# Low weight parts by an accumulating DMA instead of a GpSimd subtraction, in a two-layer hybrid decoder

## The chip, the cores and the metric

The kernel runs on one core of a Trainium2 chip. A core has a matrix engine (TensorE, PE in the profile, with its weight loads on a row of their own, PEld), a vector engine (VectorE, DVE), a scalar engine (ScalarE, ACT), GpSimd (POOL), and SyncE (SP), which here only issues DMAs. ACT and POOL can issue DMAs too. Each engine runs its own list of instructions in order and waits at semaphores for the others. The metric is the device time of one execution in microseconds; the kernel before takes 1241.17 us (median of 3 runs, 1240.09 to 1242.71).

## The reference

Two decoder layers on 512 tokens of width 1024, in float32. A layer has four groups of attention heads that share one input projection and one output projection, then a dense feed-forward network, with a norm ahead of and behind each part:

```python
for l in range(DEPTH):                      # DEPTH = 2
    h = rmsnorm(x, g_pre_mix[l])
    z = jnp.einsum('bsd,de->bse', h, w_in[l])
    z_moba, z_fox, z_fg, z_cq, z_ckv, z_kr, z_dil = jnp.split(z, SPLIT_POINTS, axis=-1)
    ...
    mix = jnp.concatenate([from_heads(o_moba), from_heads(o_fox), from_heads(o_mla),
                           from_heads(o_dil)], axis=-1)
    y = jnp.einsum('bse,ed->bsd', mix, w_out[l])
    x = x + rmsnorm(y, g_post_mix[l])
    h = rmsnorm(x, g_pre_ffn[l])
    f = jax.nn.silu(jnp.einsum('bsd,df->bsf', h, w_gate[l])) * jnp.einsum('bsd,df->bsf', h, w_up[l])
    f = jnp.einsum('bsf,fd->bsd', f, w_down[l])
    x = x + rmsnorm(f, g_post_ffn[l])
```

The latents (`z_fg`, `z_cq`, `z_ckv`, `z_kr`; 356 columns) feed the forget gates and the low-rank attention.

## The kernel before, in words

**Matmuls in three passes.** Every float32 operand of a projection is split into a high part `hi` (the value cast to `float32r`, a type that the matrix engine multiplies faster) and a low part `lo = value - hi`. `mm3` (L195 to L198) multiplies hi·hi, hi·lo and lo·hi into one PSUM bank. So each weight chunk that is loaded costs a load, a cast and a subtraction before all three passes can run.

**Weight chunks.** `weights()` (L159 to L173) makes one chunk, mostly 128 x 512 values (256 KB). SyncE loads it into a buffer `wraw` (L166; there are 5, `WRAW`), ACT casts it (L167) into `whi` or a place given by `into`, and the low part is made from `wraw` and `hi`, either on DVE (L172) or on GpSimd (L170). `wlo` and `whi` have 6 buffers each (`WSPL`). `chunk_no` counts the chunks, and every chunk whose number is a multiple of `pool_share` goes to GpSimd: every 4th in the front of a layer (`SHARE_MIX`), every 10th while attention runs (`SHARE_HEADS`), every 2nd in the first feed-forward blocks (`SHARE_FFN`), and none after them. In the two layers that makes 26 chunks: 18 `wlo`, 4 `lat_lo` (the latent projection's weights, 128 x 356), 2 `w_half`, 1 `wlate`, 1 `wfirst`. A buffer `wraw` is free for the load five chunks later when both its readers are done.

**Order of the work.** The five engines' lists come from a scheduler that runs when the kernel is built and orders the instructions by costs of its own, so a change of one instruction can move others. At the very start it is switched off for ACT, DVE and POOL, and the order is written by hand, in a string of steps "s0 a0 w0 w1 t0 s1 w2 w3 a1 s2 t1 a2 s3 t2 a3 t3" (L1027): for the four row blocks of 128 tokens, `s` is the norm's statistics (ACT L230, then two small POOL instructions for the reciprocal root, L234 and L235), `a` the scaling on DVE (L209) and the transposes on PE (`hnT`, L217), and `t` the split of the transposed rows into `h` (cast on ACT and subtraction on DVE, both L225). The steps w0 to w3 load the four chunks of the first value projection; the fourth of them is a GpSimd chunk (`wlo_185`).

**The head.** PE computes the value projection `ps_v` and the latent projection `ps_lat` of one row block after the other as `h` comes. The latents need eight weight chunks, k = 0 to 7, whose high parts are `lat_hi` and whose low parts lie in two tiles: `lat_lo_265` for k = 0 to 3 and `lat_lo_266` for k = 4 to 7. Chunks k = 3 and k = 7 are GpSimd chunks.

**Behind the head.** The projections of the head groups, attention, and the output projection `ps_out` (weights `wearly`, `wlate`, `wlo`) run interwoven. Then comes the feed-forward network: its first blocks (`ps_g`, `ps_u`) start while the last row blocks of the output projection are still closed with norms (L764 to L767), and the rest is a long chain of matmuls in which all low parts come from DVE.

Of the kernel before, what the change touches and what calls it, by code (L numbers as in the profile page):

```python
# [13 lines left out]
ALU = mybir.AluOpType  # L14
# [62 lines left out]
def f32(ap):  # L77
    return ap.bitcast(F32)
# [3 lines left out]
def decoder(ctx, tc, x, positions, w_in, b_forget, g_mla_q, w_mla_q_up, g_mla_kv, w_mla_kv_up,  # L82
            w_out, g_pre_mix, g_post_mix, w_gate, w_up, w_down, g_pre_ffn, g_post_ffn, consts, out):
    nc = tc.nc
# [71 lines left out]
    chunk_no = [0]  # L156
    pool_share = [SHARE_MIX]

    def weights(src, shape, into=None):  # L159
        raw = wp.tile([P] + shape, F32, name="wraw", tag="wraw", bufs=WRAW)  # L160
        if into is None:
            hi = wp.tile([P] + shape, F32R, name="whi", tag="whi", bufs=WSPL)
            lo = wp.tile([P] + shape, F32R, name="wlo", tag="wlo", bufs=WSPL)
        else:
            hi, lo = into
        nc.sync.dma_start(raw, src)  # L166
        nc.scalar.copy(hi, raw)  # L167
        chunk_no[0] += 1
        if pool_share[0] and chunk_no[0] % pool_share[0] == 0:
            nc.gpsimd.tensor_tensor(lo, raw, f32(hi), op=ALU.subtract)  # L170
        else:
            nc.vector.tensor_tensor(lo, raw, f32(hi), op=ALU.subtract)  # L172
        return hi, lo  # L173
# [16 lines left out]
    def weights_v(l, c0, i, into=None):  # L190
        return weights(w_cols(l, c0, 256, 2 * i, 2), [2, 256], into=into)
# [76 lines left out]
    def mixing(l, h_in, in_slots, out_slots, w_first, turns_in):  # L268
# [43 lines left out]
        def fetch_T(c0):  # L312
            return [weights(w_cols(l, c0, P, 4 * i, 4), [4, P]) for i in range(2)]
# [230 lines left out]
        def window(col):  # L544
# [7 lines left out]
        lat_hi = keep.tile([P, KD, N_LAT], F32R, name="lat_hi", tag="slotE")  # L552
        lat_lo = [slot(s, F32R, "lat_lo") for s in out_slots[1:3]]
        wl = [weights(w_in[l, k * P:(k + 1) * P, C_LAT:C_LAT + N_LAT], [N_LAT],
                      into=(lat_hi[:, k, :], lat_lo[k // 4][:, k % 4, 0:N_LAT])) for k in range(KD)]
        gains_lat = R(F32, "gqkv")
# [537 lines left out]
```

## Time and profile before

| | |
|---|---|
| median of 3 runs | 1241.17 us (1240.09 to 1242.71) |
| profiled execution | 1241.33 us |
| span of its trace | 1239.5 us |
| PE busy | 1211.5 us, 98% |
| DVE busy | 890.6 us, 72% |
| ACT busy | 666.9 us, 54% |
| POOL busy | 245.0 us, 20% |

The span is what the trace shows from the first to the last instruction; 1.8 us of the profiled execution's time lie around it. Busy times of different engines overlap. A row of a timeline gives the start and the duration in microseconds, the engine, the line, the operation with what it writes and reads, the number of like instructions in a row, and in brackets how long the engine stood idle before it and whose end it waited for. In the lines of the profile of before `ACT L167` is the cast of a weight chunk, `POOL L170` the subtraction on GpSimd and `DVE L172` the subtraction on DVE.

### The profile page before, as it was taken

What the parts mean: (1) busy time and instruction counts of PE and PEld (TensorE: products, weight loads), DVE (VectorE), ACT (ScalarE), POOL (GpSimd) and SP (SyncE); (2) the same over time, 40 slices, a digit from 0 to 9 for tenths busy, and PEclk for the clock granted to TensorE, in tenths of its full rate; (3) what the DMA queues carried; (4) which work ended last, traced back from release to release, by engine and by line L of the source; (5) the groups of instructions that cost most, each with busy time, mean ns of one, the idle gap of its engine ahead of it and who ended that gap; (6) DMA issues with size and microseconds to landing.
All of it is one profiled execution on the core that took longest, in us unless ns stands there. A gap on an engine that the chain in (4) does not pass through costs nothing.

```text
span 1239.5 us, 20756 instructions
## 1 busy us (share of the span) xinstructions
PE 1211.5 (98%) x7372; PEld 1069.6 (86%) x7372; DVE 890.6 (72%) x1802; ACT 666.9 (54%) x1453; POOL 245.0 (20%) x337
## 2 busy tenths in 40 slices
PE   8999999989999999999999999999899999999997
PEld 7878877779999999888798888778799999998886
DVE  6877877778987888533667678766788987893334
ACT  6676766754554445332547677666454444453232
POOL 3343444343000000000242434333420000000001
PEclk9999999999999999999999999999999999999999
DMA  7221242521433333533622123233224333343331
GB/s 233 76 61 43 70 117 71 162 68 35 135 96 103 111 103 94 152 95 102 186 84 52 43 69 98 73 116 106 69 69 129 111 94 103 104 117 113 102 91 71
DMA packets 158060, 121.68 MB, mean 98 GB/s; under 512 B 9090, under 2 KB 133122, under 8 KB 157956
## 3 DMA queue, kind: packets, MB, share of 16 engines
q1 hardware_dynamic: 151908, 111.55, 30.9%
q10 hardware_dynamic: 6048, 8.80, 2.7%
q8 instruction: 58, 0.95, 0.3%
q14 instruction: 46, 0.38, 0.1%
HBM read 111.93 MB, written 4.19 MB: 94 GB/s over the span
## 4 chain that ended last, share of the span: by engine, by line
PE 83%; DVE 6%; ACT 4%; issue 2%; DMA 2%; POOL 2%; ACTq 0%; DVEq 0%; POOLq 0%
PE ps L197 8%; PE ps L196 8%; PE ps L198 8%; PE ps_d L197 6%; PE ps_d L198 6%; PE ps_d L196 6%; PE ps_g L197 4%; PE ps_g L196 4%; PE ps_g L198 3%; PE ps_qk L196 3%; PE ps_s L462 3%; PE ps_qk L197 3%; PE ps_qk L198 3%; PE pT L486 2%; PE ps_o L494 1%
## 5 line engine op out<-in xcount | busy, mean ns | idle before, releaser
L172 DVE TENSOR_TENSOR wlo<-wraw,whi 128x512 fp32r<-128x512 f32 x206 | 156.2, 767 | 133.2 <-ACT whi L167 130.7
L167 ACT CAST whi<-wraw 128x512 fp32r<-128x512 f32 (+1 forms) x224 | 135.7, 620 | 170.7 <-PE ps_d L198 117.9
L895 ACT CAST whi<-wsum 128x512 fp32r<-128x512 f32 x120 | 74.3, 620 | 133.4 <-DVE wsum L901 46.5
L197 PE MATMUL ps<-sum,whi 128*128 128x256 f32 x480 | 135.8, 283 | 0.0
L196 PE MATMUL ps<-sum,whi 128*128 128x256 f32 x480 | 135.5, 282 | 0.0
L198 PE MATMUL ps<-sum,wlo 128*128 128x256 f32 x480 | 135.3, 282 | 0.0
L196 PE MATMUL ps_d<-whi,fh 128*128 128x512 f32 x288 | 112.2, 390 | 0.0
L197 PE MATMUL ps_d<-wlo,fh 128*128 128x512 f32 x288 | 112.1, 389 | 0.0
L198 PE MATMUL ps_d<-whi,fl 128*128 128x512 f32 x288 | 112.0, 389 | 0.0
L198 PE MATMUL ps<-h,wlo 128*128 128x256 f32 x360 | 101.9, 283 | 0.0
L197 PE MATMUL ps<-h,whi 128*128 128x256 f32 x360 | 101.9, 283 | 0.0
L196 PE MATMUL ps<-h,whi 128*128 128x256 f32 x360 | 101.8, 283 | 0.0
L477 POOL TENSOR_SCALAR pr<-pr,den 128x128 f32<-128x128 f32 (+3 forms) x128 | 75.7, 608 | 115.1 <-DVE den L474 85.2
L198 PEld LDWEIGHTS ps<-sum,wlo 128*128 128x128 f32 x480 | 91.9, 192 | 0.0
L196 PEld LDWEIGHTS ps<-sum,whi 128*128 128x128 f32 x480 | 91.8, 191 | 0.0
L197 PEld LDWEIGHTS ps<-sum,whi 128*128 128x128 f32 x480 | 91.8, 191 | 0.0
L896 DVE TENSOR_TENSOR wlo<-wsum,whi 128x512 fp32r<-128x512 f32 x120 | 80.9, 683 | 9.5 <-ACT whi L895 8.4
L197 PE MATMUL ps_g<-h,whi 128*128 128x512 f32 (+1 forms) x224 | 81.3, 363 | 5.8 <-DVE h L225 5.8
L196 PE MATMUL ps_g<-h,whi 128*128 128x512 f32 (+1 forms) x224 | 81.1, 363 | 0.9 <-ACT h L225 0.8
L198 PE MATMUL ps_g<-h,wlo 128*128 128x512 f32 (+1 forms) x224 | 80.6, 360 | 0.0
L895 ACT CAST whi<-wraw 128x512 fp32r<-128x512 f32 x90 | 55.8, 620 | 42.6 <-PE ps L197 27.5
L196 PE MATMUL ps_qk<-h,whi 128*128 128x512 f32 x192 | 76.5, 398 | 0.0
(330 smaller groups left out, 3437.8 us busy)
## 6 DMA issues: line engine op xcount, KB each, us to landing
wraw<-in_w_gate_dram SPq DMA_DIRECT2D x88, 256.0 KB, 3.5
wraw<-in_w_up_dram SPq DMA_DIRECT2D x88, 256.0 KB, 3.1
wraw<-in_w_down_dram SPq DMA_DIRECT2D x88, 256.0 KB, 2.9
wraw<-in_w_in_dram SPq DMA_DIRECT2D x72, 256.0 KB, 3.1
wraw<-in_w_out_dram SPq DMA_DIRECT2D x32, 256.0 KB, 2.8
xt<-in_x_dram SPq DMA_DIRECT2D x16, 256.0 KB, 3.7
rope_b<-rope_a ACTq DMA_DIRECT2D x64, 64.0 KB, 2.0
wraw<-in_w_in_dram SPq DMA_DIRECT2D x16, 178.0 KB, 2.9
```

Source lines behind the costliest of these rows:

```text
L167: nc.scalar.copy(hi, raw)
L172: nc.vector.tensor_tensor(lo, raw, f32(hi), op=ALU.subtract)
L196: nc.tensor.matmul(ps, a_hi, b_hi, start=start, stop=False)
L197: nc.tensor.matmul(ps, a_hi, b_lo, start=False, stop=False)
L198: last_mm[0] = nc.tensor.matmul(ps, a_lo, b_hi, start=False, stop=stop)
L462: nc.tensor.matmul(ps[:, 0:w], a[:, qt * P:(qt + 1) * P], b[:, 0:w], start=i == 0, stop=i == n - 1)
L477: nc.gpsimd.tensor_scalar(p, p, den[:, t - qa:t - qa + 1], 1.0, op0=ALU.mult, op1=ALU.mult)
L486: nc.tensor.transpose(pt[:, i * P:(i + 1) * P], pr[:, offs[qt] + kt * P:offs[qt] + (kt + 1) * P], ident)
L494: nc.tensor.matmul(o, v, mh, start=kt == 0, stop=False)
L895: nc.scalar.copy(hi, raw)
L896: nc.vector.tensor_tensor(lo, raw, f32(hi), op=ALU.subtract)
```

## The change

The subtraction on GpSimd goes. In its place ACT writes the negated value of the raw chunk, cast to `float32r`, into the low tile (so -hi), and GpSimd issues a DMA that reads the raw chunk and adds it to what stands in the low tile: raw - hi. All 26 chunks take this way; those of DVE stay. Everything from L159 on stands four lines lower in the changed kernel.

```diff
@@ -156,6 +156,10 @@
     chunk_no = [0]
     pool_share = [SHARE_MIX]
 
+    def low_by_dma(lo, raw):
+        nc.scalar.mul(lo, raw, -1.0)
+        nc.gpsimd.dma_start(lo, raw, accum_op=ALU.add)
+
     def weights(src, shape, into=None):
@@ -167,7 +171,7 @@
         nc.scalar.copy(hi, raw)
         chunk_no[0] += 1
         if pool_share[0] and chunk_no[0] % pool_share[0] == 0:
-            nc.gpsimd.tensor_tensor(lo, raw, f32(hi), op=ALU.subtract)
+            low_by_dma(lo, raw)
         else:
             nc.vector.tensor_tensor(lo, raw, f32(hi), op=ALU.subtract)
         return hi, lo
```

The scheduler puts the new instructions into the engines' lists, and with that others move. Three places follow.

First, ACT in the head, from the cast of the last chunk of the value projection on. `wraw_279` and `wraw_295` are the latent chunks k = 3 and k = 7 before, `wraw_280` and `wraw_297` the same now; `hnT_219` and `hnT_220` is the first half of row block 2, `hnT_247` and `hnT_248` that of row block 3, and the next `hnT` after each the second half. Before:

```order
L167 CAST whi_184<-wraw_183 128x512
L230 ACTIVATE hn_206,ss_205<-xt_201 128x512
...
L167 CAST lat_hi_264<-wraw_279 128x356
L167 CAST lat_hi_264<-wraw_283 128x356
L167 CAST lat_hi_264<-wraw_287 128x356
L225 CAST h_123<-hnT_219 128x4x128
...
L167 CAST lat_hi_264<-wraw_295 128x356
L167 CAST whi_554<-wraw_553 128x512
L167 CAST whi_560<-wraw_559 128x512
L225 CAST h_123<-hnT_247 128x4x128
L225 CAST h_124<-hnT_252 128x4x128
```

And now:

```order
L171 CAST whi_184<-wraw_183 128x512
L160 ACTIVATE wlo_185<-wraw_183 128x512
L234 ACTIVATE hn_207,ss_206<-xt_202 128x512
...
L171 CAST lat_hi_265<-wraw_280 128x356
L160 ACTIVATE lat_lo_266<-wraw_280 128x356
L229 CAST h_123<-hnT_220 128x4x128
...
L171 CAST lat_hi_265<-wraw_297 128x356
L229 CAST h_123<-hnT_248 128x4x128
L160 ACTIVATE lat_lo_267<-wraw_297 128x356
L229 CAST h_124<-hnT_253 128x4x128
```

The three negations stand between the casts; the one of k = 7 stands between the two casts of row block 3, where before it was POOL's work behind the cast of k = 7.

Second, PE in the head, where it comes to the latent chunk k = 3 and to the transposes of row block 3. Before (`lat_lo_265` holds k = 0 to 3, `lat_lo_266` k = 4 to 7):

```order
L196 MATMUL ps_lat_330<-lat_hi_264,h_123 128x356
L197 MATMUL ps_lat_330<-lat_lo_265,h_123 128x356
L198 MATMUL ps_lat_330<-lat_hi_264,h_125 128x356
L196 MATMUL ps_lat_330<-lat_hi_264,h_124 128x356
L197 MATMUL ps_lat_330<-lat_lo_266,h_124 128x356
...
L217 MATMUL hnT_247<-cst_79,hn_234 128x128 x4
L197 MATMUL ps_v_365<-wlo_185,h_124 128x256
L198 MATMUL ps_v_365<-whi_184,h_126 128x256
L217 MATMUL hnT_252<-cst_79,hn_235 128x128 x4
L197 MATMUL ps_lat_330<-lat_lo_266,h_124 128x356
```

And now (`lat_lo_266` holds k = 0 to 3, `lat_lo_267` k = 4 to 7):

```order
L200 MATMUL ps_v_368<-whi_184,h_124 128x256
L201 MATMUL ps_lat_333<-lat_lo_266,h_123 128x356
L221 MATMUL hnT_248<-cst_79,hn_235 128x128 x4
L202 MATMUL ps_lat_333<-lat_hi_265,h_125 128x356
L200 MATMUL ps_lat_333<-lat_hi_265,h_124 128x356
L221 MATMUL hnT_253<-cst_79,hn_236 128x128 x4
L201 MATMUL ps_lat_333<-lat_lo_267,h_124 128x356
...
L200 MATMUL ps_lat_395<-lat_hi_265,h_123 128x356
L201 MATMUL ps_lat_395<-lat_lo_266,h_123 128x356
L201 MATMUL ps_lat_333<-lat_lo_267,h_124 128x356
```

The pass with the low part of k = 3 now stands right ahead of the transposes of row block 3, where before most of the passes of k = 4 to 6 and of the value projection lay between them; the last row shown is the pass with the low part of k = 7.

Third, ACT in the output projection of layer 0, around one chunk of `w_out` (`wraw_2945` before, `wraw_2953` now). Before:

```order
L541 CAST mix_2632<-mixf_2782 128x256
L488 CAST ptb0_95<-pT_2886 128x384
L756 COPY park_2739<-ps_out_2830 128x512
L167 CAST whi_2946<-wraw_2945 128x512
L167 CAST whi_2952<-wraw_2951 128x512
```

And now:

```order
L171 CAST whi_2954<-wraw_2953 128x512
...
L760 COPY park_2747<-ps_out_2773 128x512
L160 ACTIVATE wlo_2955<-wraw_2953 128x512
L171 CAST whi_2961<-wraw_2960 128x512
...
L545 CAST mix_2640<-mixf_2790 128x256
...
L492 CAST ptb0_95<-pT_2894 128x384
L760 COPY park_2747<-ps_out_2838 128x512
```

The cast and the negation of this chunk stand ahead of the copy of the next `ps_out` bank, where before the cast stood behind it.

## Rows read from the trace of the kernel before

**Rows 1.** The page's first lines: busy time of each engine with its share of the span and its instructions.

```profile
span 1239.5 us, 20756 instructions
PE 1211.5 (98%) x7372; PEld 1069.6 (86%) x7372; DVE 890.6 (72%) x1802; ACT 666.9 (54%) x1453; POOL 245.0 (20%) x337
```

**Rows 2.** The waits of PE by what it waited for: total us, times, longest us.

```profile
PE ps_g L197 <- DVE h L225: 5.8, 4, 1.9
...
PE ps_out L197 <- POOL wlo L170: 0.4, 1, 0.4
```

**Rows 3.** The GpSimd subtraction, L170, by the tile that it writes (count, shortest/median/longest ns), and one row of the cast of a weight chunk on ACT from the groups by line (count, busy us, mean ns).

```profile
L170 POOL TENSOR_TENSOR wlo<-wraw,whi x18: 1282/1298/1832, 12.7 to 873.7; 128x512 fp32r<-128x512 f32 x18
...
L167 ACT CAST lat_hi<-wraw 128x356 fp32r<-128x356 f32 x16 | 7.3, 489 | 3.5 <-DMA wraw<-in_w_in_dram 3.3
L167 ACT CAST whi<-wraw 128x512 fp32r<-128x512 f32 (+1 forms) x224 | 135.7, 620 | 170.7 <-PE ps_d L198 117.9
```

**Rows 4.** The timeline of the head: ACT, POOL, DVE, then PE.

```profile
11.53 1.13 ACT L167 CAST whi<-wraw 128x512 fp32r<-128x512 f32 x2
17.34 1.65 ACT L167 CAST lat_hi<-wraw 128x356 fp32r<-128x356 f32 x4
21.83 0.49 ACT L167 CAST lat_hi<-wraw 128x356 fp32r<-128x356 f32 x1 [1.21 <-DMA wraw<-in_w_in_dram]
25.58 1.07 ACT L225 CAST h<-hnT 128x512 fp32r<-128x512 f32 x2
...
12.73 1.29 POOL L170 TENSOR_TENSOR wlo<-wraw,whi 128x512 fp32r<-128x512 f32 x1
18.45 1.04 POOL L170 TENSOR_TENSOR lat_lo<-wraw,lat_hi 128x356 fp32r<-128x356 f32 x1
22.40 0.95 POOL L170 TENSOR_TENSOR lat_lo<-wraw,lat_hi 128x356 fp32r<-128x356 f32 x1 [2.91 <-ACT lat_hi L167]
...
14.31 0.97 DVE L172 TENSOR_TENSOR lat_lo<-wraw,lat_hi 128x356 fp32r<-128x356 f32 x2
...
14.07 0.39 PE L197 MATMUL ps_v<-wlo,h 128*128 128x256 f32 x1 [0.18 <-POOL wlo L170]
21.11 0.28 PE L198 MATMUL ps_v<-whi,h 128*128 128x256 f32 x1
21.23 0.28 PE L196 MATMUL ps_v<-whi,h 128*128 128x256 f32 x1
22.31 0.63 PE L217 MATMUL hnT<-cst,hn 128*128 128x128 f32 x4
24.21 0.32 PE L196 MATMUL ps_lat<-lat_hi,h 128*128 128x356 f32 x1
24.37 0.33 PE L197 MATMUL ps_lat<-lat_lo,h 128*128 128x356 f32 x1
```

**Rows 5.** DMA issues of the first 30 us (the first two rows), and of the whole run (the others): KB each, median us from issue to landing.

```profile
wraw<-in_w_in_dram SPq DMA_DIRECT2D x8, 256.0 KB, 3.8
wraw<-in_w_in_dram SPq DMA_DIRECT2D x8, 178.0 KB, 3.0
...
rope_b<-rope_a ACTq DMA_DIRECT2D x64, 64.0 KB, 2.0
out_dram<-xt SPq DMA_DIRECT2D x8, 256.0 KB, 2.0
gain<-in_g_post_ffn_dram ACTq DMA_DIRECT2D x4, 256.0 KB, 5.9
```

**Rows 6.** A stretch of the head: busy time and instructions of PE, PEld, DVE, ACT and POOL, the granted clock, the busy share of the DMA engines, GB/s.

```profile
20.00:25.00 5.00, 4.75 (x34) 4.34 (x33) 4.22 (x8) 1.73 (x4) 0.95 (x1) 1.00 0.82 209
```

**Rows 7.** The timeline where a GpSimd chunk of the first projections of layer 0 is made, and the PE row that reads it first.

```profile
43.11 1.46 POOL L170 TENSOR_TENSOR wlo<-wraw,whi 128x512 fp32r<-128x512 f32 x1 [4.13 <-ACT whi L167]
...
52.51 0.39 PE L198 MATMUL ps_qk<-h,wlo 128*128 128x512 f32 x1
```

**Rows 8.** The timeline of the chunk `wraw_2945` of the output projection in layer 0.

```profile
238.82 1.67 ACT L167 CAST whi<-wraw 128x512 fp32r<-128x512 f32 x3
...
239.53 1.29 POOL L170 TENSOR_TENSOR wlo<-wraw,whi 128x512 fp32r<-128x512 f32 x1 [0.55 <-ACT whi L167]
...
240.88 0.50 PE L197 MATMUL ps_out<-wlo,mix 128*128 128x512 f32 x1 [0.37 <-POOL wlo L170]
```

**Rows 9.** The timeline at the start of the feed-forward network of layer 0.

```profile
266.62 1.28 POOL L170 TENSOR_TENSOR w_half<-wraw,w_half 128x512 fp32r<-128x512 f32 x1 [1.23 <-ACT w_half L167]
...
267.19 1.25 DVE L764 TENSOR_TENSOR park<-park,gain 128x512 f32<-128x512 f32 x1 [0.66 <-ACT jk L230]
...
268.37 0.68 DVE L225 TENSOR_TENSOR h<-hnT,h 128x512 fp32r<-128x512 f32 x1
...
268.97 0.67 DVE L764 TENSOR_TENSOR park<-park,gain 128x512 f32<-128x512 f32 x1
269.10 0.39 PE L197 MATMUL ps_g<-h,whi 128*128 128x256 f32 x1 [1.03 <-DVE h L225]
...
272.67 0.39 PE L197 MATMUL ps_g<-h,whi 128*128 128x256 f32 x1 [1.87 <-DVE h L225]
```

**Rows 10.** The timeline of PE where the attention of layer 0 begins.

```profile
55.78 0.44 PE L198 MATMUL ps_qup<-whi,sp_lo 128*128 128x384 f32 x1 [0.23 <-DVE sp_lo L627]
57.09 0.44 PE L659 MATMUL ps_qup<-whi,q_stk 128*128 128x384 f32 x1 [0.87 <-DVE q_stk L633]
```

## The prediction

> **What bounds the kernel now.** I read the page's first lines before anything else. PE is busy for 1211.5 us, 98% of the span, and POOL for 20% [rows 1], so a faster or slower POOL moves the end only through PE's idle time, some 28 us in all. Next I read the waits of PE by releaser: PE waited for a low part of GpSimd once for 0.4 us at `ps_out` [rows 2], and once for 0.18 us at `ps_v` in the head [rows 4]. So the subtraction on POOL, 1.3 us a chunk [rows 3], is hidden nearly everywhere. The question is not what it cost, but whether what takes its place is hidden too. For that I took each of the 26 chunks and compared the end of its low part on POOL with the first PE row that reads it. Four have no room: `wlo_185`, k = 3 and k = 7 of the latents, all three in the head [rows 4], and one chunk of the output projection [rows 8]. The tightest of the other 22 ends at 44.57 and is read at 52.51 [rows 7], 7.9 us later.
>
> **The new step and its price.** For a chunk, 1.3 us on POOL are replaced by a negation on ACT and a transfer. No row shows this negation; its nearest relative is the cast, 0.62 us for 128 x 512 and 0.49 us for 128 x 356 [rows 3], 0.41 us each when four follow each other (1.65 us, rows 4). I take those, and in a queue of ACT 0.62 and 0.41. The transfer's time L, from the end of the negation to the landing, is the main unknown, as no transfer of before is issued by GpSimd or adds. Low end: 2.0 us, a transfer from SBUF to SBUF of 64 KB and a store of 256 KB [rows 5]. High end: 5.9 us, the slowest group of 256 KB loads there. I take 4.0: the loads of 178 KB of just this stretch take 3.0 us [rows 5], with the DMA engines 82% busy [rows 6], and I add 1 us, an estimate with no row behind it, for reading the destination as well and for GpSimd's issuing.
>
> The Trainium skill, "DMA: Bandwidth & Descriptors", section "Anatomy of one DMA — SWDGE (gpsimd) path", gives for a transfer issued by GpSimd about 2.0 us plus the bytes at 436 GB/s, which makes an estimate of 2.4 us for 178 KB; by it the loss in the head below would be its floor. The loads of this stretch took 3.0 us for those bytes, and that section speaks of no accumulation, so I keep 4.0.
>
> **The head.** The order shows what now hangs on what. ACT's statistics of row block 3 end at 17.3 as before [rows 4]; three casts (1.24 us) and the negation of k = 3 (0.41) bring it to 18.9, and k = 3 lands at 18.9 + L = 22.9. PE comes to that pass at about 21.3 (by the order it has then, against before at 24.37, twelve latent passes of 0.16 us and eight transposes, 1.2 us, fewer, and one value pass more), or at 22.6 if it had to wait for `wlo_185`: that lands at 13.2 + L = 17.2 (ACT's casts end at 12.65, rows 4, and one negation), where PE is at 15.9 (14.07, and four value passes, eight transposes and one latent pass). Either way PE waits for k = 3. Right behind that pass stand the transposes of row block 3, and ACT's next instructions need them: 0.16 for the pass, 0.6 for four transposes, 0.54 for the cast of half of `h` (two take 1.07 in rows 4), then the negation of k = 7, 0.41. That is 18.9 + L + 1.7 = 20.6 + L, and k = 7 lands at 20.6 + 2L = 28.6. The latency counts twice, since the second transfer can't begin before the first has released PE. Before, PE began the pass of k = 7 at 24.37. Now it has three more passes of the value projection ahead of that (0.12 each, 21.11 to 21.23 in rows 4) and two more of the latents (0.16 each), so the same work would be done at 25.1. Loss: 28.6 - 25.1 = 3.5 us; in general 2L - 4.5.
>
> For a small L there is a floor: k = 7 itself is cast no earlier than 21.83 to 22.3, for it waits for its load [rows 4]. Behind it: half `h`, negation, half `h` on ACT (1.5), 0.68 for `h` on DVE (as in rows 9), 0.49 for the low part of k = 6 (two take 0.97, rows 4), 25.0; PE needs that at 24.2. Floor of the loss: 0.8 us, reached below L of about 2.7.
>
> Queues that the edit reaches here: on POOL the reciprocal root of row block 2 stands behind the DMA of `wlo_185`, but its sum comes from ACT about a microsecond after the negation, so it doesn't get later. On SP the load of k = 4 needs the buffer of `wlo_185`'s chunk, free at 17.2 instead of 14.02; with 3.0 us for the load its cast is at 20.3, and k = 7 follows by 23.1, half a microsecond ahead of the cast of `h` behind it.
>
> **Elsewhere.** The chunk of the output projection: before, its cast stood behind a copy of `ps_out`, POOL ended at 240.82, and PE waited 0.37 us [rows 8]. Now cast and negation come ahead of the copy of the next bank, and I count over 6 us of PE's matmuls between them and the reader. That covers L = 4: -0.4 us. If the cover were gone, the low part would land at 239.5 + 0.6 + 4 = 244.1 instead of 240.8, a loss of 3.3.
>
> The start of the feed-forward network: with POOL's subtraction at 266.62 running, DVE's L764 at 267.19 takes 1.25 us, the next one 0.67 [rows 9]. The subtraction goes, so `h` comes 0.58 us earlier and PE's wait of 1.03 shrinks; but the next wait, 1.87 us at 272.67, hangs on another chain and takes part of it back. I count half, 0.25 us, for each of two layers: -0.5 (bounds 0 and -1.2).
>
> Where attention begins, PE waits 0.23 and 0.87 us for DVE's `sp_lo` and `q_stk` [rows 10]. If PE arrives later there, as the head's loss makes it, these waits shrink by up to 1.1; how far that chain is late itself I can't read, so -0.5 (bounds 0 and -1.1).
>
> The other 22 chunks: POOL's 1.3 us go, 0.62 + L come; with 7.9 us to spare this holds up to an L of 8.6. ACT gets 22 x 0.62 + 4 x 0.49 = 15.6 us, on an engine that is 54% busy [rows 1]; outside the head I cost it at nothing, and where a cast is late by 0.62 us PE would lose at most that.
>
> Sum against the profiled execution: 1241.33 + 3.5 - 0.4 - 0.5 - 0.5 = 1243.4. That execution lies 0.16 us above the median of 1241.17, so against the median: 1243.3 us. A difference of 0.2%, 2.5 us, is about what a measurement of this kernel can tell from no change; +2.1 is inside it, not by much.
>
> **The rivals.** First, the transfer is cheap: L below 3, so the head loses 0.8 to 1.5 us and the gains of 1.4 pay for it: 1240.6 to 1241.3. For it speaks the 2.0 us for 64 KB and for a store; against it the load of the DMA engines in just this stretch.
>
> Second, on the slower side: the transfer is dear, because it moves each byte twice (destination in, sum out) where the engines are 82% busy. With twice 3.0 us, L = 6, the head loses 7.5, and the time is 1247.3. The place is the double wait of k = 3 and k = 7; it decides for slower from L = 4.2 on (2L - 4.5 - 1.4 = 2.5). Against it speaks that in SBUF to SBUF transfers, which don't share the memory's channel, the only row is as short as 2.0.
>
> Third, faster: DVE gains more without POOL beside it than I count. PE waits for DVE's `h` four times, 5.8 us in all [rows 2]. If each shrinks by 0.58 us, 2.3, and the waits of 1.1 and 0.4 go whole, with the head at its floor, the result is 0.8 - 3.8 = -3.0, 1238.2. Against it: two of the four hang on the other chain.
>
> **How the numbers follow.** L between 3 and 5, 1241.3 to 1245.3: 0.55, of which 0.33 lies below L = 4.2. Cheap: 0.15. Dear, L above 5, or the same loss from a cover that fails in the output projection: 0.18. Faster: 0.12. So within 0.2%: 0.33 + 0.15 = 0.48; slower: 0.22 + 0.18 = 0.40; faster: 0.12. The range 1240 to 1247.3 takes in the first two cases and the dear one up to L = 6, half of its chance: 0.55 + 0.15 + 0.09, about 0.8.
>
> **What would show it.** In the profile of the changed kernel: the median from issue to landing of the transfers `wlo<-wraw` and `lat_lo<-wraw`; waits of PE for those DMAs, at the passes `ps_lat` of k = 3 and k = 7 and perhaps once at `ps_v`, within the first 30 us, some 3.5 us together; no wait of `ps_out` on such a chunk; L764 at the feed-forward start at 0.67 us. What would make me wrong: a wait on such a DMA outside the head, or an L so small that no PE row of the head waits for it, or ACT late for PE because of its 15.6 us.

## The result and the profile after

The changed kernel takes 1258.45 us (median of 4 runs, 1256.96 to 1259.13), against 1241.42 us for the kernel before on the same chip (4 runs). The ratio is 1.0137, interval 1.0125 to 1.015: slower by 17.0 us. The forecast was 1243.3 us with a range that ended at 1247.3. The profiled execution took 1259.13 us; the lines below are from its trace.

The page's first lines, the counterpart of [rows 1]:

```profile
span 1257.3 us, 20819 instructions
PE 1216.2 (97%) x7372; PEld 1075.1 (86%) x7372; DVE 878.2 (70%) x1802; ACT 678.4 (54%) x1479; POOL 230.1 (18%) x337
```

POOL and DVE have less to do, ACT 11.5 us more, and PE does the same 7372 matmuls in 4.7 us more of busy time. So the loss of 17.8 us of span is 13 us of idle PE and nearly 5 us of slower PE.

PE's longest waits, by releaser (total us, times, longest us), the counterpart of [rows 2]:

```profile
PE ps_g L201 <- DVE h L229: 6.2, 4, 2.7
PE ps_lat L201 <- DMA lat_lo<-wraw: 4.9, 1, 4.9
PE ps_o L498 <- DVE mixf L538: 3.2, 1, 3.2
...
PE ps_g L200 <- ACT h L229: 2.3, 4, 1.1
PE hnT L221 <- DVE h L229: 1.8, 1, 1.8
...
PE ps_v L201 <- DMA wlo<-wraw: 1.0, 1, 1.0
...
PE ps_qk L202 <- DMA wlo<-wraw: 0.8, 1, 0.8
```

Three of these waits are put down to one of the new transfers, 6.7 us together; a fourth, of 0.71 us in the head, belongs to them as well, as the next rows show. The others are for DVE and ACT.

The head: ACT, POOL's issues of DMAs, PE, then one weight load of PE; the counterpart of [rows 4]:

```profile
12.49 0.63 ACT L160 ACTIVATE wlo<-wraw 128x512 fp32r<-128x512 f32 x1
18.04 0.50 ACT L160 ACTIVATE lat_lo<-wraw 128x356 fp32r<-128x356 f32 x1
24.23 0.58 ACT L229 CAST h<-hnT 128x512 fp32r<-128x512 f32 x1 [1.30 <-PE hnT L221]
24.72 0.51 ACT L160 ACTIVATE lat_lo<-wraw 128x356 fp32r<-128x356 f32 x1
25.01 0.34 ACTq L588 DMA_DIRECT2D cst<-in_consts_dram  x1
...
13.43 1.08 POOL L161 DMA_DIRECT2D wlo<-wraw  x1 [0.83 <-ACT wlo L160]
25.52 0.85 POOL L161 DMA_DIRECT2D lat_lo<-wraw  x1 [5.73 <-ACT lat_lo L160]
...
17.26 0.39 PE L201 MATMUL ps_v<-wlo,h 128*128 128x256 f32 x1 [1.02 <-DMA wlo<-wraw]
23.33 0.43 PE L201 MATMUL ps_lat<-lat_lo,h 128*128 128x356 f32 x1 [0.71 <-DVE lat_lo L176]
32.87 0.67 PE L201 MATMUL ps_lat<-lat_lo,h 128*128 128x356 f32 x1 [4.86 <-DMA lat_lo<-wraw]
...
23.33 0.19 PEld L201 LDWEIGHTS ps_lat<-lat_lo,h 128*128 128x128 f32 x1 [0.92 <-DMA lat_lo<-wraw]
```

The first transfer is 4.1 us from the end of its negation (13.12) to PE's start (17.26). The pass of k = 3 begins at 23.33. Its row names DVE, whose subtraction for another chunk happened to end then; the weight load of the same pass names the transfer, issued at 18.86 and landed 4.4 us later, at 23.26, which is 4.7 us from the end of its negation. The half of `h` behind it is cast at 24.23, and the negation of k = 7 ends at 25.23. Up to here the timeline is that of the forecast, some half a microsecond later. Then k = 7 lands only at 32.87, 7.6 us behind its negation. Half a microsecond ahead of its issue stands another on ACT: the load of the kernel's constants.

DMA issues between 24 and 34 us, KB each and us from issue to landing:

```profile
wraw<-in_w_in_dram SPq DMA_DIRECT2D x3, 256.0 KB, 6.6
cst<-in_consts_dram ACTq DMA_DIRECT2D x1, 589.0 KB, 7.2
...
lat_lo<-wraw POOLq DMA_DIRECT2D x1, 178.0 KB, 7.3
```

These five took between 6.6 us (the median of the three loads) and 7.3 us. Of the whole run the median of the new transfers is shorter:

```profile
wlo<-wraw POOLq DMA_DIRECT2D x18, 256.0 KB, 4.2
lat_lo<-wraw POOLq DMA_DIRECT2D x4, 178.0 KB, 4.4
```

The stretches around that wait: length, busy time of PE, PEld, DVE, ACT and POOL (instructions), the granted clock, DMA share, GB/s:

```profile
25.00:28.00 3.00, 2.26 (x13) 1.76 (x11) 2.34 (x5) 1.07 (x3) 0.85 (x1) 1.00 1.07 270
28.00:32.80 4.80, 0.00 (x1) 0.00 (x0) 0.69 (x1) 0.62 (x1) 0.45 (x1) 0.64 0.76 204
32.80:35.00 2.20, 2.13 (x7) 2.14 (x8) 0.29 (x2) 1.14 (x3) 0.16 (x1) 0.50 0.36 102
35.00:37.00 2.00, 2.00 (x11) 2.00 (x10) 0.56 (x1) 0.48 (x4) 1.44 (x4) 0.71 0.74 188
37.00:39.00 2.00, 2.00 (x16) 2.00 (x15) 0.95 (x2) 0.43 (x1) 1.49 (x3) 1.00 0.62 167
```

While PE stands idle the granted clock falls from 1.00 to 0.50, that is from 2.4 to 1.2 GHz, and it is back at 1.00 only at about 36 us. In the 2.2 us from 32.8 on PE is busy nearly all the time and gets 7 matmuls done. The idle time is paid once by itself and then again in slow matmuls.

**Where the 17 us came from.** In both traces I took the start of the same piece of PE's work (the n-th matmul into a tile of that name) and subtracted before from after. The table shows this delay, in microseconds, at points through the program, for the changed kernel and for the experiments below.

| point (its time before) | after | head only | head undone | add on GpSimd | FFN only | FFN + first projections | copy, no add | all on DVE |
|---|---|---|---|---|---|---|---|---|
| first `ps_qk`, end of the head (42.5) | 9.4 | 10.8 | 0.0 | 2.2 | 0.3 | -0.3 | 6.4 | -0.2 |
| first `ps_s` (59.1) | 7.5 | 8.9 | -0.7 | 0.3 | 0.0 | -1.2 | 4.5 | -1.8 |
| late `ps_qk`, layer 0 (189.0) | 5.6 | 9.1 | -1.5 | 2.1 | -0.1 | -0.8 | 3.7 | -3.0 |
| output projection, layer 0 (246.4) | 11.1 | 9.6 | 2.8 | 5.0 | -0.1 | -0.7 | 8.6 | -3.4 |
| feed-forward, layer 0, under way (279.2) | 13.3 | 9.6 | 3.8 | 7.0 | 2.2 | 2.2 | 9.8 | -2.5 |
| layer boundary passed (624.3) | 15.0 | 9.8 | 5.3 | 6.3 | 2.4 | 4.5 | 10.1 | -3.4 |
| output projection, layer 1 (876.0) | 16.0 | 9.3 | 6.1 | 7.8 | 2.8 | 4.1 | 10.9 | -4.0 |
| last matmuls (1232.1) | 17.2 | 9.4 | 7.3 | 9.2 | 2.1 | 4.9 | 11.1 | -4.5 |

In the column of the changed kernel: the head loses 9.4; 3.8 come back before the late `ps_qk`; the piece up to the output projection of layer 0 loses 5.5, the feed-forward start of layer 0 2.3, the layer boundary 1.7, the rest of layer 1 2.2.

The second piece, layer 0 around 200 us. ACT, then POOL's issue, then PE:

```profile
180.92 0.62 ACT L171 CAST whi<-wraw 128x512 fp32r<-128x512 f32 x1 [0.88 <-PE ps_qk L201]
199.42 0.63 ACT L160 ACTIVATE wlo<-wraw 128x512 fp32r<-128x512 f32 x1
...
200.35 0.89 POOL L161 DMA_DIRECT2D wlo<-wraw  x1 [4.06 <-ACT wlo L160]
...
201.52 0.48 PE L498 MATMUL ps_o<-pta,v 128*128 128x512 f32 x1 [3.23 <-DVE mixf L538]
203.73 0.79 PE L202 MATMUL ps_qk<-h,wlo 128*128 128x512 f32 x1 [0.78 <-DMA wlo<-wraw]
```

The cast of this chunk is at 180.92, its negation at 199.42, because it stands 28 rows further down in ACT's list (rows of the instruction order, with their numbers):

```
254 L171 CAST whi_2391<-wraw_2390 128x512
...
282 L160 ACTIVATE wlo_2392<-wraw_2390 128x512
```

Before, GpSimd made this low part at 175.29, 0.07 us after the cast had ended, and PE had a dozen `ps_qk` passes to run while `mixf` was made. Now those passes need a low part whose negation begins only at 199.42. In PE's new list `ps_o` stands ahead of them, and PE waits 3.2 us for `mixf`, then for the transfer, and then runs at half clock:

```profile
200.00:204.00 4.00, 1.48 (x4) 0.76 (x5) 3.49 (x5) 2.64 (x6) 2.20 (x2) 0.93 0.38 66
204.00:206.00 2.00, 1.72 (x4) 0.90 (x5) 2.00 (x5) 1.61 (x3) 0.00 (x0) 0.50 0.41 131
206.00:208.00 2.00, 2.00 (x8) 1.71 (x8) 1.91 (x6) 1.14 (x3) 0.00 (x0) 0.50 0.49 141
208.00:210.00 2.00, 2.00 (x6) 1.61 (x5) 0.16 (x1) 0.26 (x3) 0.37 (x1) 0.50 0.36 129
```

The third piece, the start of the feed-forward network of layer 0, SyncE, ACT, DVE, then PE and a stretch, the counterpart of [rows 9]:

```profile
273.80 0.37 SPq L170 DMA_DIRECT2D wraw<-in_w_up_dram  x1
...
277.50 0.62 ACT L171 CAST w_half<-wraw 128x512 fp32r<-128x512 f32 x1 [1.13 <-DMA wraw<-in_w_up_dram]
...
278.78 0.69 DVE L768 TENSOR_TENSOR park<-park,gain 128x512 f32<-128x512 f32 x1 [1.09 <-ACT jk L234]
...
279.27 0.39 PE L200 MATMUL ps_g<-h,whi 128*128 128x256 f32 x1 [0.75 <-ACT h L229]
280.13 0.38 PE L201 MATMUL ps_g<-h,whi 128*128 128x256 f32 x1 [0.47 <-DVE h L229]
284.51 0.39 PE L201 MATMUL ps_g<-h,whi 128*128 128x256 f32 x1 [2.69 <-DVE h L229]
...
286.00:288.00 2.00, 2.00 (x11) 2.00 (x11) 2.00 (x4) 0.14 (x1) 0.00 (x0) 0.50 0.36 100
```

The DVE instruction that took 1.25 us beside GpSimd takes 0.69, and the wait of 1.03 us is 0.47, both as forecast. But the wait for ACT's `h` grew from 0.24 to 0.75, the last wait from 1.87 to 2.69, and with that wait the clock fell to 0.50 again. ACT's cast of `h` stands behind a cast of `w_half`, and that one waits for its load. SyncE issued the load at 273.80, when a `wlo` transfer had landed: the raw chunk's buffer is now free only when the transfer has read it. Before, the load went out at 262.03, behind a subtraction of DVE; with PE 11.1 us late here its counterpart would be 273.1. So the load is 0.7 us late, and ACT's `h` with it by half a microsecond. No run tests this chain by itself.

### The profile page after: what moved, and what is told of

The parts are those of the page before. It is cut to its first block, busy times and chain, and to the rows that moved or that the text cites. A ratio compares the mean times of both kernels' runs of the same rounds, so it can differ in the third digit from the quotient of the medians.

```text
span 1257.3 us, 20819 instructions
## 1 busy us (share of the span) xinstructions
PE 1216.2 (97%) x7372; PEld 1075.1 (86%) x7372; DVE 878.2 (70%) x1802; ACT 678.4 (54%) x1479; POOL 230.1 (18%) x337
## 4 chain that ended last, share of the span: by engine, by line
PE 84%; ACT 4%; DMA 4%; DVE 4%; POOL 2%; issue 2%; DVEq 0%; POOLq 0%; ACTq 0%
PE ps L201 8%; PE ps L200 8%; PE ps L202 8%; PE ps_d L200 6%; PE ps_d L201 6%; PE ps_d L202 6%; PE ps_g L201 4%; PE ps_g L200 3%; PE ps_g L202 3%; PE ps_s L466 3%; PE ps_qk L200 3%; PE ps_qk L202 3%; PE ps_qk L201 3%; PE pT L490 2%; PE ps_o L498 2%
## 5 line engine op out<-in xcount | busy, mean ns | idle before, releaser
L176 DVE TENSOR_TENSOR wlo<-wraw,whi 128x512 fp32r<-128x512 f32 x206 | 148.1, 725 | 137.9 <-ACT whi L171 135.7
L202 PE MATMUL ps_qk<-h,wlo 128*128 128x512 f32 x192 | 76.9, 402 | 0.8 <-DMA wlo<-wraw 0.8
```

What stands on the lines that cost most here:

```text
L202: last_mm[0] = nc.tensor.matmul(ps, a_lo, b_hi, start=False, stop=stop)
```

## The experiments

Theory 1: each stage pays for itself; the head by the late transfer of k = 7 and by the clock, the rest by where the two new steps stand. Theory 2: all is the head's, and the later losses follow from it.

**Head undone.** The three chunks of the head on GpSimd's subtraction again:

```diff
         if pool_share[0] and chunk_no[0] % pool_share[0] == 0:
-            low_by_dma(lo, raw)
+            if chunk_no[0] > 12:
+                low_by_dma(lo, raw)
+            else:
+                nc.gpsimd.tensor_tensor(lo, raw, f32(hi), op=ALU.subtract)
```

> The changed kernel with the three GpSimd chunks of the head (wlo_185 and the latent chunks k = 3 and k = 7 of layer 0) made by the GpSimd subtraction again; the other 23 by negation and DMA. Theory 1, each stage pays for itself: the head's 9.4 us of loss go, and so do the 3.8 us that a late head got back before the output projection; what is left is the output projection of layer 0 (+5.5), the two feed-forward starts (+2.3, +1.0), the layer boundary (+1.7) and attention of layer 1 (+1.3), so 1253 us. Theory 2, the loss is all the head's, and the later losses are its consequences: 1241 to 1244 us.

Measured: 1250.17 us, ratio 1.0069 (1.0054 to 1.0084). The head's delay is 0.0, and 7.3 us stay. The time is below the 1253 us of theory 1 and far above the 1241 to 1244 of theory 2.

**Head only.** The reverse:

```diff
         if pool_share[0] and chunk_no[0] % pool_share[0] == 0:
-            low_by_dma(lo, raw)
+            if chunk_no[0] <= 12:
+                low_by_dma(lo, raw)
+            else:
+                nc.gpsimd.tensor_tensor(lo, raw, f32(hi), op=ALU.subtract)
```

> The reverse: only the three chunks of the head by negation and DMA, the other 23 by the GpSimd subtraction. Theory 1: the head loses 9.4 us at the first ps_qk as in the changed kernel, some 3.8 us come back by the output projection, 1247 us. Theory 2: near the changed kernel's 1258 us.

Measured: 1250.60 us, ratio 1.0071 (1.0056 to 1.0086). The head alone ends with 9.4 us, the rest alone with 7.3; together 16.7 of the 17.2 in the table. Theory 2 is out: the rest loses with no delay ahead of it, and a delayed head makes nothing else lose. Only 1.9 us come back behind the head (10.8 to 8.9, where attention begins); my 3.8 us had half of it from elsewhere.

**The negation without the transfer.**

```diff
         nc.scalar.mul(lo, raw, -1.0)
-        nc.gpsimd.dma_start(lo, raw, accum_op=ALU.add)
+        nc.gpsimd.tensor_tensor(lo, raw, f32(lo), op=ALU.add)
```

> The negation on ACT stays in all 26 chunks, but GpSimd adds the raw chunk itself (1.3 us) in place of the DMA. If the transfer's time is what costs: the head and the waits for DMAs lose nothing, about 1243 us, with the ACT part of the loss at the feed-forward starts left (h later by 0.5 us in each layer, 1 to 2 us). If the negations on ACT and the order that they bring are what costs: over 1250 us.

Measured: 1253.68 us (1250.45 to 1255.40), ratio 1.0099 (1.0082 to 1.0116); its profiled execution is the fastest of the four, 3.2 us ahead of their median, so its column in the table ends at 9.2, and where the others lose their further microseconds is not known. The head loses 2.2 in place of 9.4: there it is the transfer. Behind the head it loses 7.0 us, where the kernel with the head undone loses 7.3; the pieces differ (2.9 against 4.3 up to the output projection of layer 0), so that the sums agree is in part chance. But a loss of this kind is there without any transfer. The place around 200 us shows why. ACT, POOL, PE of this kernel:

```profile
176.48 1.14 ACT L171 CAST whi<-wraw 128x512 fp32r<-128x512 f32 x2
195.96 0.63 ACT L160 ACTIVATE wlo<-wraw 128x512 fp32r<-128x512 f32 x1
...
196.73 1.26 POOL L161 TENSOR_TENSOR wlo<-wraw,wlo 128x512 fp32r<-128x512 f32 x1 [3.90 <-ACT wlo L160]
...
198.04 0.50 PE L202 MATMUL ps_qk<-h,wlo 128*128 128x512 f32 x1 [3.22 <-POOL wlo L161]
```

The negation stands 18.3 us behind the end of its cast here too, and PE waits 3.2 us for what follows it.

**The negation on GpSimd, with the transfer.**

```diff
-        nc.scalar.mul(lo, raw, -1.0)
+        nc.gpsimd.tensor_scalar(lo, raw, -1.0, None, op0=ALU.mult)
         nc.gpsimd.dma_start(lo, raw, accum_op=ALU.add)
```

> The changed kernel with the negated high part written by GpSimd in place of ACT, the DMA as it is. ACT's list then has nothing of the change. If the negations in ACT's list made the losses outside the head (output projection of layer 0, feed-forward starts, boundary; 7.3 us with the head undone): those go, and with the head's loss of 9 to 10 us the kernel takes about 1251 us. If they come from the DMA itself, its time or GpSimd's issue: 1258 us or more.

Measured: 1264.50 us, ratio 1.0179 (1.0162 to 1.0196), the slowest of all. My expectation of 1251 was wrong as a sum: the GpSimd negation takes 1.49 to 1.93 us, the head loses 11.5, and the layer boundary 4.0. But at the place around 200 us its delay stays at 9.8 to 9.9, so nothing is lost there; the last row is from the output projection behind it:

```profile
185.58 1.93 POOL L160 TENSOR_SCALAR wlo<-wraw 128x512 fp32r<-128x512 f32 x1
187.81 0.89 POOL L161 DMA_DIRECT2D wlo<-wraw  x1 [0.30 <-POOL wlo L160]
...
252.70 0.50 PE L201 MATMUL ps_out<-wlo,mix 128*128 128x512 f32 x1 [1.99 <-DMA wlo<-wraw]
```

With the negation out of ACT's list the loss around 200 us goes, with the transfer left in. Together with the run before, that shows the cause there: where the negation stands in ACT's list, not the time of the transfer. At the output projection this run pays another price: PE waits 2.0 us for the transfer of the chunk that had no room before, [rows 8], and the delay goes from 10.2 to 11.8.

**DMA kept out of attention and the output projection.** The head's three chunks go back to GpSimd's subtraction, and of the other 23 those made while attention and the output projection run:

```diff
         if pool_share[0] and chunk_no[0] % pool_share[0] == 0:
-            low_by_dma(lo, raw)
+            if chunk_no[0] > 12 and pool_share[0] != SHARE_HEADS:
+                low_by_dma(lo, raw)
+            else:
+                nc.gpsimd.tensor_tensor(lo, raw, f32(hi), op=ALU.subtract)
```

> The changed kernel with the head's three chunks and the chunks made while attention and the output projection run (every 10th) on GpSimd's subtraction again; DMA only in the other first projections and in the first feed-forward blocks. If the 4.3 us that the run with the head undone loses between the last ps_qk chunks and the output projection of layer 0 come from the negation that stands 28 rows behind its cast in ACT's list: they go, nothing is lost there, and the kernel takes 1244 to 1246 us, near the run with DMA in the feed-forward blocks alone (1245.4). If they come from the feed-forward or the first projections: 1250 us as with the head undone.

Measured: 1246.19 us, ratio 1.0037 (1.0024 to 1.0050). Nothing is lost between 189 and 246 us (-0.8 to -0.7 in the table), as expected.

**DMA in the feed-forward start alone.**

```diff
         if pool_share[0] and chunk_no[0] % pool_share[0] == 0:
-            low_by_dma(lo, raw)
+            if pool_share[0] == SHARE_FFN:
+                low_by_dma(lo, raw)
+            else:
+                nc.gpsimd.tensor_tensor(lo, raw, f32(hi), op=ALU.subtract)
```

> Only the chunks of the first feed-forward blocks (8 of 26) by negation and DMA, the others by the GpSimd subtraction. If each stage pays for itself: the losses at the two feed-forward starts, 1.1 and 1.3 us in the run with the head undone, and nothing elsewhere: about 1244 us. If they were consequences of the earlier stages: 1242 us. If the gain that I predicted there (DVE without GpSimd beside it) is real when nothing else changes: 1241 us.

Measured: 1245.40 us (10 runs), ratio 1.0022 (1.0013 to 1.0032). The delay comes at the start of layer 0's blocks, 2.2 us. So my gain there is a loss. The difference to the run above is the layer boundary: 0.3 us here, 2.3 there, which puts that loss on the chunks of layer 1's first projections. By which of their steps, no run separates.

**The constants' load moved.** It is issued behind the copy of the first latents, which comes after the pass of k = 7:

```diff
-            nc.scalar.copy(lat[t][:, 0:N_LAT], ps[:, 0:N_LAT])
+            copied = nc.scalar.copy(lat[t][:, 0:N_LAT], ps[:, 0:N_LAT])
+            if l == 0 and t == 0:
+                with tc.issue_after(copied.ins):
+                    nc.scalar.dma_start(cst[:, K_TRI:], consts[:, K_TRI:])
...
-        if l == 0:
-            with tc.issue_after(normed[0].ins):
-                nc.scalar.dma_start(cst[:, K_TRI:], consts[:, K_TRI:])
```

> The changed kernel with the 589 KB load of constants moved from behind the last cast of h (25.0 us) to behind the copy of the first latents, which comes after the pass of k = 7. If the transfer for k = 7 took 7.3 us from issue to landing because that load was issued half a microsecond ahead of it: its time falls to 4 to 5 us, the wait of PE for it from 4.9 to about 2 us, the head's loss at the first ps_qk from 9.4 to 5 or 6, and the kernel takes about 1254 us. If the weight loads beside it, or the transfer itself, made it long: 7 us and 1258 us.

Measured: 1254.94 us, ratio 1.0105 (1.0084 to 1.0126). From its DMA issues between 24 and 40 us:

```profile
wraw<-in_w_in_dram SPq DMA_DIRECT2D x3, 256.0 KB, 4.2
...
lat_lo<-wraw POOLq DMA_DIRECT2D x1, 178.0 KB, 4.8
```

The transfer for k = 7 takes 4.8 us in place of 7.3, the weight loads beside it 4.2 in place of 6.6, and PE waits 2.4 in place of 4.9. The head's delay is 6.8 us. So the constants' load made the difference between 4.8 and 7.3.

**A plain copy in place of the addition.** The low tile holds the raw chunk, the subtraction is left out; the order on PE is the same:

```diff
-        nc.gpsimd.dma_start(lo, raw, accum_op=ALU.add)
+        nc.gpsimd.dma_start(lo, raw)
```

> The changed kernel with a plain copy by GpSimd's DMA in place of the accumulating one, in the same order on every engine; the subtraction is left out, the low tile holds the raw chunk. I put 1 us of L down to reading the destination and to GpSimd's issue. If the addition has that price: the median from issue to landing falls from 4.2 to about 3 us and k = 7 from 7.3 to about 6, and the kernel takes 1256 us. If the addition costs nothing: 4.2 us, 7.3 us and 1258 us.

Measured: 1252.63 us, ratio 1.0090 (1.0075 to 1.0105). Its DMA issues, of the whole run:

```profile
wlo<-wraw POOLq DMA_DIRECT2D x18, 256.0 KB, 2.9
lat_lo<-wraw POOLq DMA_DIRECT2D x4, 178.0 KB, 3.1
```

Against 4.2 and 4.4 the addition costs 1.3 us a transfer. A part of it is GpSimd's issue, 0.60 us against 0.89 in the medians of line L161. The transfer for k = 7, issued between 24 and 34 us, takes 5.5 us in place of 7.3, and the constants' load 5.4 in place of 7.2. The head loses 6.4 in place of 9.4.

**Work in place of the wait.** 30 matmuls of a zero tile, whose product adds nothing, ahead of the pass of k = 7:

```diff
             for k in range(KD):
+                if l == 0 and t == 0 and k == KD - 1:
+                    for _ in range(30):
+                        nc.tensor.matmul(ps[:, 0:N_LAT], ptb[0][:, 0:P], wl[k - 1][0], start=False, stop=False)
                 mm3(ps[:, 0:N_LAT], hh(k, ts), hl(k, ts), *wl[k], k == 0, k == KD - 1)
```

> The changed kernel with 30 more matmuls of a zero tile (their product adds nothing) in the accumulation of ps_lat of the first row block, right ahead of the pass of k = 7, 4.9 us of work where PE stood idle for 4.86 us. If the clock's fall after that idle time is a part of the head's loss: the granted clock stays at 1.00 from 28 to 40 us, the loss at the first ps_qk is about 6 us in place of 9.4, and the kernel takes 1255 us. If the fall has nothing to do with idle time, or costs nothing: 1258 us as before.

Measured: 1256.42 us, ratio 1.0117 (1.0102 to 1.0132). The same stretch as above:

```profile
28.00:32.80 4.80, 4.78 (x30) 4.47 (x28) 1.39 (x2) 1.24 (x2) 0.77 (x2) 1.00 0.86 222
32.80:35.00 2.20, 2.18 (x13) 2.18 (x14) 1.25 (x5) 1.50 (x6) 1.92 (x5) 1.00 0.42 105
```

With PE busy the clock stays at 1.00, and 13 matmuls run where 7 ran. The delay at the first `ps_qk` is 8.2 us in place of 9.4. So the clock's part of the head's loss is 1.2 us in the changed kernel, a third of the 3.4 I expected; in the run with the head alone, where the granted clock was at 0.50 until 39 us, it is some 2.6 (10.8 less 8.2).

**All low parts on DVE.** Neither GpSimd nor a transfer:

```diff
         if pool_share[0] and chunk_no[0] % pool_share[0] == 0:
-            low_by_dma(lo, raw)
+            nc.vector.tensor_tensor(lo, raw, f32(hi), op=ALU.subtract)
```

> All 26 low parts by DVE's subtraction, nothing on GpSimd and no DMA. If it is enough that the subtraction leaves GpSimd: not slower than before, 1240 to 1243 us. If DVE is full where these chunks are made (head, output projection): 1243 to 1248 us.

Measured: 1235.83 us (1233.69 to 1237.43), ratio 0.9941 (0.9925 to 0.9958): faster than both kernels. DVE is busy for 893 us, 3 more than before, though it has 26 subtractions more, of 0.69 us each for the 18 `wlo`; so its other instructions took some 15 us less, an estimate from these numbers. The table shows small gains from the start of attention on, and 1.3 us lost again in the feed-forward start of layer 0 (-3.8 at its first pass, -2.5 under way).

**GpSimd kept in the feed-forward start alone.**

```diff
         if pool_share[0] and chunk_no[0] % pool_share[0] == 0:
-            low_by_dma(lo, raw)
+            if pool_share[0] == SHARE_FFN:
+                nc.gpsimd.tensor_tensor(lo, raw, f32(hi), op=ALU.subtract)
+            else:
+                nc.vector.tensor_tensor(lo, raw, f32(hi), op=ALU.subtract)
```

> All low parts by DVE but the 8 in the first feed-forward blocks, which stay on GpSimd as before. The run with all on DVE (1235.8) is 3.8 us ahead of before at the first feed-forward block of layer 0 and loses 1.3 of them there, and gains 0.4 at the start of layer 1's. If DVE is full there: the 1.3 us stay, 1234.5 to 1235.5 us. If the loss there has another cause: 1236 us.

Measured: 1237.02 us (10 runs, 1234.79 to 1240.59), ratio 0.9966 (0.9954 to 0.9977). In its profiled execution, its fastest, the 1.3 us are not lost. Over all runs it is not ahead of the kernel with all on DVE, whose interval its own overlaps. Inconclusive, and I would take the simpler one.

## Why the prediction was wrong

The forecast fell short by 15.2 us. By the table, 5.9 of that lie in the head, which lost 9.4 where the sum had 3.5, and 9.2 behind it, where 7.8 were lost and the sum had a gain of 1.4. Two steps failed, one in each.

**In the head the mechanism was right and one term of it was mis-sized.** The head was the place with the largest single loss, by the mechanism that the forecast described: ACT's negation of k = 7 waits for transposes that stand behind the pass of k = 3, and so the latency counts twice. Each step up to the issue of k = 7 came within 0.7 us: the first transfers 4.1 us (`wlo`) and 4.7 (k = 3) against L = 4.0, the pass of k = 3 at 23.3 against 22.9, the negation of k = 7 finished at 25.2 against 24.6. The failed step is "k = 7 lands at 20.6 + 2L": it uses one L for the transfers of k = 3 and k = 7. The second took 7.6 us. With that, the same sum gives 25.2 + 7.6 - 25.1 = 7.7 for the head, of the 9.4 measured. The load of the constants, issued at 25.06 before as well, was in the trace I had; I took the loads of 178 KB from the whole stretch of 30 us for a measure of what k = 7 would meet at 25 us. The run with that load moved shows the price, 2.5 us of transfer and 2.6 us of delay.

**The allowance of 1 us was nearly right.** It had no row behind it. Against the plain copy, which GpSimd issues too, the addition cost 1.3 us a transfer, the longer issue included. The estimate worked out from the Trainium skill, "DMA: Bandwidth & Descriptors", section "Anatomy of one DMA — SWDGE (gpsimd) path", was 2.4 us for 178 KB, and by the same terms it is 2.6 for 256 KB. The plain copies took 3.1 and 2.9, the accumulating ones 4.4 and 4.2. So the estimate from the Trainium skill is near for a copy here, and 1.6 to 2.0 us short for an addition.

**The clock was not in the sum.** The granted clock stood at 1.00 in nearly every row of before, so I priced a wait of PE at its length. The trace of before had one place that says otherwise, at the start of layer 1's feed-forward network: behind a wait of 1.88 us for `h`, which ended at 882.28, the granted clock was 0.50 in the stretch from 884 to 886 us. In the changed kernel the waits in the head, around 200 us and at the feed-forward start of layer 0 each have a clock of 0.50 in the microseconds behind them. In the head that was 1.2 us, measured by filling the wait. In the other places it is seen in the rows and was not measured apart.

**The step on the other 22 chunks, costed at nothing, failed**, and by more than any bound I had given it: with the head undone all 23 chunks behind it, the one of the output projection among them, cost 7.3 us. I took the slack from the end of GpSimd's work to the first reader, 7.9 us or more, and put the negation right behind the cast. For one chunk in layer 0 the list of ACT put it 28 rows behind, 18 us later, and that could be read from the order before any run. The piece with this place in it cost 4.3 us (-1.5 to 2.8 with the head undone). The rest is the layer boundary and the feed-forward starts; for the boundary no step is named by a run. One sign that the forecast named for being wrong stands in the profile: a wait for such a transfer outside the head, 0.78 us at `ps_qk`. The slack was taken from the old order and the new step's position was not looked up. My check of three places in the order was a check of the places that were tight before.

**At the output projection** the step was right as far as it went: the wait of 0.37 us [rows 8] is gone. The loss came in front of it. The run with the negation on GpSimd shows how thin the cover is: there PE waits 2.0 us for this chunk.

**At the feed-forward start** the mechanism held: DVE's instruction took 0.69 us, and the wait of 1.03 became 0.47. The sign of the term was wrong, since the load ahead of ACT's `h` was left out, whose buffer now comes free with a transfer: PE waits for ACT's `h` 0.5 us longer, the next chain ends 0.8 us later, and the clock falls. Instead of -0.5 for both layers together, the run with DMA there alone is slower by 0.2%.

**At the beginning of attention** the recovery was larger than my 0.5 us and its bound of 1.1: 1.9 (9.4 to 7.5). With the head undone 0.7 us come back there too, so not all of it is the late head's.

**The rivals.** The transfer was dear where it mattered, as the second rival had it, at 7.6 us. Its ground was that each byte moves twice. No run measures that by itself; the addition as a whole accounts for 1.8 us (7.3 to 5.5 with the plain copy), the constants' load for 2.5 (7.3 to 4.8). At L = 6 it forecast 1247.3, and even its time was short by 11 us, because outside the head the only loss that any case had was the 3.3 us of a cover that fails at the output projection. The third rival's idea was worth more than its 0.12: without GpSimd's subtractions the run with all on DVE is 0.6% faster. Whether that comes from DVE's other instructions, shorter by some 15 us together, or from subtractions of 0.7 in place of 1.3 us, no run separates. Giving the work to ACT and the DMA engines loses more than that.

## What to carry to other kernels

When a step is split in two, look up where each half stands in its engine's list for every place, not only for the tight ones; slack measured in the old order says nothing about a step that the scheduler has moved 28 rows. For a transfer on the critical path, take the latency from what is in flight at its own microsecond, and ask which large load is issued just ahead of it. A wait of the matrix engine costs more than its length where the clock falls behind it, and work that is hidden can be cheapest on the busier engine: DVE at 72% took all 26 chunks and the kernel became faster.

## What the runs showed of the hardware

The accumulating transfer from SBUF to SBUF took 4.2 us in the median from issue to landing for 256 KB, a plain copy by the same queue 2.9, and GpSimd spent 0.89 against 0.60 us on the issue. A load of 589 KB, three of 256 KB and an accumulating transfer of 178 KB that were under way together took 6.6 to 7.3 us each, by the median of the three; with plain copies the load of 589 KB itself took 5.4 us in place of 7.2. After 4.9 us in which PE did nothing the granted clock was at 0.50, and it stayed there for 3.2 us of full work (32.87 to 36.10); with PE busy over the same time it stayed at 1.00.
